# Elementwise work from GpSimd to VectorE and ScalarE, and the later modulation loads on another queue

## The chip, the cores and the metric

The kernel runs on one core of a Trainium2 chip. Its time is the device time of one execution in microseconds (us). Five engines run their own instruction streams in order and wait for one another by semaphores: TensorE (PE; its weight loads are listed as PEld), VectorE (DVE), ScalarE (ACT), GpSimd (POOL) and SyncE (SP), which only issues DMA transfers here. GpSimd issues transfers too, from a queue of its own.

## The reference, cut to what matters

Two transformer blocks, one after the other, on 512 tokens of width 1024 in float32. The first has a recurrent mixer and a sparse attention (projections, rope, softmax branches), then a mixture of 64 experts. The second has two layers of feed-forward, mixer, feed-forward. Both are modulated: vectors computed from a condition `c` scale and shift every normalised activation and scale every residual.

```python
c_act = silu(c)                                  # first block
sh1, sc1, g1, sh2, sc2, g2 = split(c_act @ w_ada[l] + b_ada[l], 6)
h = rmsnorm(x, norm1_g[l]) * (1 + sc1) + sh1
x = x + g1 * (concat([recurrent(h), sparse_attention(h)]) @ w_out[l])
x = x + g2 * moe_ffn(rmsnorm(x, norm2_g[l]) * (1 + sc2) + sh2)

c_act = silu(c_2)                                # second block, two layers
mod = (c_act @ w_mod[l] + b_mod[l]).reshape(9, 1024)
h = modulate(x, g_norm[l, 0], mod[0], mod[1])
x = x + 0.5 * mod[2] * swiglu(h, w_ffn1_gu[l], w_ffn1_down[l])
h = modulate(x, g_norm[l, 1], mod[3], mod[4])
x = x + mod[5] * hybrid_mixer(h, ...)            # window attention, linear recurrence, short convolution
h = modulate(x, g_norm[l, 2], mod[6], mod[7])
x = x + 0.5 * mod[8] * swiglu(h, w_ffn2_gu[l], w_ffn2_down[l])
return rmsnorm(x, g_final)
```

## The kernel before

Matrix products are done to nearly full float32 precision with three passes: every operand is split into a rounded high part and the rest (`split`, lines 164 to 167: ScalarE makes `whi`, VectorE the rest `wlo`), and `mm3` (L160 to L162) adds high by high, high by rest and rest by high. So each piece of 128x1024 weights costs one copy on ScalarE and one subtraction on VectorE before TensorE can use it. Raw weights come over SyncE's queue into three buffers `wraw`; `whi` and `wlo` have three buffers each.

The program runs through four phases. Phase A loads the tokens and normalises them. Phase B makes the projections, the levels of the recurrence (L726 to L790, many small VectorE products on `QP` and `KS`), rope (L386 to L393) and attention (`nsa_cmp`, `nsa_att`). Phase C is the mixture of experts, ended by `moe_end`. Phase D is the second block: `ffn`, `mixer`, `ffn`, twice. In what follows the four feed-forwards are called by layer and place: (0,0), (0,2), (1,0), (1,2).

A modulation vector needs a sum over eight blocks of 128x1024 weights, each scaled by a column of the condition. `mod_acc` (L181) does that: a load of 512 KB into `mraw` (two buffers), then the scaled sum into `macc`, and after eight of them `mod_cols` (L199) adds over the partitions on TensorE (16 small matmuls, L205) and puts the vector into a column tile. It is a generator, and yields after every second block; `tick` (L1442) advances it by one yield at set places of the program: after each pair of column groups in `ffn`, after each slice of `down`, and in phase B after each step of the projections. In phase B (`b_mods`, seven vectors, 56 loads) it runs with `pool=True`: VectorE multiplies the block in place (L189) and GpSimd adds it to the sum (L191). In phase D it runs with `pool=False`: VectorE multiplies and adds in one instruction (L195). Feed-forwards (0,0) and (1,0) carry six vectors each (48 loads), (0,2) carries three (24 loads), (1,2) none.

The order of the instructions on each engine isn't that of the code: a scheduler arranges them ahead of time, by when it takes them to be ready, and `after(ins)` keeps what is issued inside it behind an instruction. `tick` issues its work behind `self.hold`. Before the change `hold` is the last instruction of a normalisation (L1508), so all of a feed-forward's modulation may start at once and is limited by the two `mraw` buffers.

GpSimd also does other elementwise work: the cosine product of rope (L391), a scaling in `hg_norm` (L821), the softmax scaling of every second branch in `nsa_att` (L883) and every second head group in `swa` (L1776), the scaling of `xT` at the end of the experts (L1407), and the running sum of squares of `sq_add` (L1470) for the next normalisation. The page calls the last 256-column part of each feed-forward or output projection `down` with `last`: it is done in two halves of the tokens, and the next normalisation of the first half runs beside the second. It is called the tail here.

Of the kernel before, what the change touches and what calls it, by code (L numbers as in the profile page):

```python
# [19 lines left out]
D = 1024  # L20
# [121 lines left out]
class Kern:  # L142
# [21 lines left out]
    def split(self, src, hi, lo, eng=None):  # L164

        self.copied = self.nc.scalar.copy(hi, src)  # L166
        self.nc.vector.tensor_tensor(lo, src, hi.bitcast(F32), OP.subtract)  # L167
# [13 lines left out]
    def mod_acc(self, src, cact, col0, pool=False):  # L181

        nc = self.nc
        acc = self.m4.tile([128, 1024], F32, name="macc", tag="macc", bufs=3)
        for k in range(8):
            w = self.m4.tile([128, 1024], F32, name="mraw", tag="mraw", bufs=2)
            nc.sync.dma_start(w, src[k * 128:(k + 1) * 128, col0:col0 + 1024])
            if pool:
                nc.vector.tensor_scalar(w if k else acc, w, cact[:, k:k + 1], None, op0=OP.mult)  # L189
                if k:  # L190
                    nc.gpsimd.tensor_tensor(acc, acc, w, OP.add)  # L191
            elif k == 0:
                nc.vector.tensor_scalar(acc, w, cact[:, 0:1], None, op0=OP.mult)
            else:
                nc.vector.scalar_tensor_tensor(acc, w, cact[:, k:k + 1], acc, op0=OP.mult, op1=OP.add)  # L195
            if k % 2:
                yield None
        yield acc
# [164 lines left out]
    def b_consts(self):  # L363
# [10 lines left out]
        nc.gpsimd.tensor_copy(self.cmpm[:].rearrange("p a b -> p (a b)"), tmp[:, 1152:1408])  # L374
# [11 lines left out]
    def rope(self, dst, src):  # L386
        nc = self.nc
        ps = self.bank("pj")
        nc.tensor.matmul(ps, self.rot, src, start=True, stop=True)
        t1 = self.mid.tile([128, S], F32, name="rt", tag="rt", bufs=1)  # L390
        nc.gpsimd.tensor_tensor(t1, src, self.cos, OP.mult)  # L391
        nc.vector.tensor_tensor(dst, ps, self.sin, OP.mult)
        nc.vector.tensor_tensor(dst, dst, t1, OP.add)  # L393

    def b_mods(self):

        yield from self.mod_sub(0, 0, pool=True)
        cols, rows = [], []
        for n in (3, 4, 2, 5):
            for v in self.mod_acc(self.p["w_ada"][0], self.cact, n * D, pool=True):  # L400
                if v is None:
                    yield
# [292 lines left out]
    def hg_inputs(self, win):  # L695
# [14 lines left out]
        with self.after(self.hold):  # L710
            self.b_consts()
        for c in range(2):
# [98 lines left out]
    def hg_norm(self, Gt):  # L811
# [6 lines left out]
        for i in range(4):  # L818
            ov = self.ohg[:, i].rearrange("p (h e) -> p h e", h=4)
            nc.vector.tensor_tensor(ov, ov, ss[:, i, :, None].to_broadcast([128, 4, 128]), OP.mult)  # L820
            nc.gpsimd.tensor_tensor(Gt[:, i], Gt[:, i], ng, OP.mult)  # L821
# [34 lines left out]
    def nsa_att(self, i, g, pct, qr):  # L856
# [11 lines left out]
        for b in range(2):  # L868
# [14 lines left out]
            (nc.gpsimd if b else nc.vector).tensor_tensor(pv, pv, sm[:, :, None].to_broadcast([128, 4, nk]), OP.mult)  # L883
# [444 lines left out]
    def moe_end(self, A, B):  # L1328
# [73 lines left out]
        for h, ps in enumerate((b0, b1)):  # L1402
# [3 lines left out]
            for k in range(0, KT, 4):  # L1406
                nc.gpsimd.tensor_tensor(x[:, k:k + 4], x[:, k:k + 4], t[:, None, :].to_broadcast([128, 4, 256]), OP.mult)  # L1407
# [5 lines left out]
    def mod_sub(self, l, s, pool=False):  # L1413
# [4 lines left out]
        for n in range(3):  # L1418
            col0 = (3 * s + n) * D
            acc = None  # L1420
            for v in self.mod_acc(src, self.cact2, col0, pool):
# [36 lines left out]
    def sq_add(self, k, h):  # L1458
# [10 lines left out]
        elif k < KT - 1:  # L1469
            nc.gpsimd.tensor_tensor(self.ssq, self.ssq, t, OP.add)  # L1470
# [54 lines left out]
    def ffn(self, gu, dn, G, late):  # L1525
# [3 lines left out]
        for gi, nf in enumerate((8, 8, 6)):  # L1529
            n = 0  # L1530
            for pr in range(nf // 2):
# [7 lines left out]
                for j in range(2):  # L1539
# [6 lines left out]
                    n += 1  # L1546
                if n == 4:
# [5 lines left out]
    def down(self, dn, f0, order, G, last):  # L1553
# [6 lines left out]
        for h in range(2 if last else 1):  # L1560
            N = 256 if last else S
            hs = slice(h * 256, h * 256 + N)
            for dp in range(4):
# [17 lines left out]
                for j in range(2):  # L1581
                    k = 2 * dp + j
                    nc.vector.scalar_tensor_tensor(self.xT[:, k, hs], ps[j], G[:, k:k + 1], self.xT[:, k, hs],  # L1583
                                                   op0=OP.mult, op1=OP.add)
# [160 lines left out]
    def swa(self, l, i, q, kk, v, swab):  # L1745
# [27 lines left out]
        for g in range(2):  # L1773
            gp = slice(g * 64, (g + 1) * 64)
            pv = pp[g][:, :, 0:nk]
            (nc.gpsimd if g else nc.vector).tensor_tensor(pv, pv, sm[:, 4 * g:4 * g + 4, None].to_broadcast([128, 4, nk]), OP.mult)  # L1776
# [14 lines left out]
    def phase_d(self):  # L1791
# [6 lines left out]
        for l in range(2):  # L1798
            for s in range(3):
# [3 lines left out]
                self.mg, late = None, self.mods(todo)  # L1803
                if n > 1:
# [33 lines left out]
def body(tc, p, dbg=None, stop=None):  # L1838
    K = Kern(tc, p, dbg, stop)
    PS = bass.MemoryType.PSUM  # L1840
    with tc.tile_pool(name="cst", bufs=1) as K.cp, \
# [6 lines left out]
        K.modc, K.mg, K.hold = {}, None, None  # L1848
        K.banks, K.pj, K.mt = dict(pj=2, sc=3, tr=2, pv=1), "pj", "sc"
# [50 lines left out]
```

## Time and profile before

| | |
|---|---|
| median of 3 runs | 3233.39 us (3231.85 to 3245.57) |
| the profiled execution | 3237.47 us, its span 3235.5 us |
| TensorE busy | 3081.7 us, 95% of the span |
| VectorE busy | 1910.3 us, 59% |
| ScalarE busy | 1237.5 us, 38% |
| GpSimd busy | 507.8 us, 16% |
| mean granted TensorE clock | 0.978 of full speed |

The span is the time from the first to the last instruction; the execution's own time lies 2 us above it. A busy TensorE is not one at its peak: a matmul that runs at half the clock, or whose operands come late, counts as busy for longer. So beside the idle time one has to look at the granted clock, and at how long like work takes in different places. The stages by time: phase A to 56 us, phase B to 520, experts to 1262, the end of the experts to 1300; feed-forwards from 1300, 1889, 2277 and 2860, the two mixers from 1704 and 2674.

### The profile page before, as it was taken

The page shows a single profiled execution, that of the slowest core. Times are in us where ns is not written, and L with a number is a line of the kernel's source. Part 1 is how long each engine was busy: PE and PEld are TensorE (multiplying, and loading weights), DVE is VectorE, ACT ScalarE, POOL GpSimd, SP SyncE. Part 2 cuts the span into 40 slices and gives each one's busy share as a digit, 9 for nine tenths or more (in the row PEclk, how much of TensorE's full clock was granted, in tenths as well). Part 3 has the DMA queues.
Part 4 walks back from the last instruction along what each step waited for, and adds up shares of the span by engine and source line. Part 5 has one row for each costly group of instructions (what it writes and reads, how often), then busy time and mean ns, then how long its engine had stood idle before and what let it go on. Part 6 is the DMA issues. An engine that isn't in the chain of part 4 may idle for free.

```text
span 3235.5 us, 40712 instructions
## 1 busy us (share of the span) xinstructions
PE 3081.7 (95%) x15628; PEld 2347.8 (73%) x15629; DVE 1910.3 (59%) x2962; ACT 1237.5 (38%) x1984; POOL 507.8 (16%) x348
## 2 busy tenths in 40 slices
PE   6998998999999996999999999999999999999999
PEld 5876577555555553777887787888777887788888
DVE  6776757877777766764355674335664355653335
ACT  5123455544454544322245432224322245442223
POOL 0255511222333322100020100001000020100001
PEclk9998899999999998999999999999999999999999
DMA  6555336999899997664243254223664243233223
GB/s 243 165 161 169 98 109 222 315 352 337 301 328 345 331 327 229 214 222 137 93 132 91 91 189 163 91 92 119 204 221 144 93 133 89 79 105 104 96 87 105
DMA packets 317575, 576.58 MB, mean 178 GB/s; under 512 B 49488, under 2 KB 252048, under 8 KB 292800
## 3 DMA queue, kind: packets, MB, share of 16 engines
q1 hardware_dynamic: 294000, 527.27, 47.8%
q0 software_dynamic: 21296, 44.56, 5.6%
q8 instruction: 125, 2.05, 0.3%
q10 hardware_dynamic: 2080, 2.10, 0.2%
q14 instruction: 74, 0.61, 0.1%
HBM read 550.84 MB, written 28.39 MB: 179 GB/s over the span
## 4 chain that ended last, share of the span: by engine, by line
PE 74%; DMA 12%; DVE 8%; issue 3%; ACT 2%; POOL 1%; SPq 0%; DVEq 0%; POOLq 0%; ACTq 0%
PE ps_fm L162 9%; PE ps_fm L161 9%; PE ps_fm L160 9%; DMA mraw<-in_w_mod_dram 8%; PE ps_dn L1322 6%; PE ps_dn L160 5%; PE ps_dn L162 5%; PE ps_dn L161 5%; PE ps_gu L160 3%; PE ps_gu L161 3%; PE ps_gu L162 3%; DVE macc L195 2%; PE ps_tr L1292 2%; PE ps_pj L161 1%; DMA wraw<-in_w_exp_gu_dram 1%
## 5 line engine op out<-in xcount | busy, mean ns | idle before, releaser
L167 DVE TENSOR_TENSOR wlo<-wraw,whi 128x1024 fp32r<-128x1024 f32 x480 | 577.6, 1208 | 570.6 <-ACT whi L166 562.8
L166 ACT CAST whi<-wraw 128x1024 fp32r<-128x1024 f32 x480 | 487.4, 1018 | 857.8 <-PE ps_fm L161 365.9
L160 PE MATMUL ps_fm<-dhh,whi 128*128 128x512 f32 (+1 forms) x1808 | 676.3, 376 | 19.7 <-ACT whi L166 11.6
L162 PE MATMUL ps_fm<-dhh,wlo 128*128 128x512 f32 (+1 forms) x1808 | 666.6, 377 | 15.4 <-DVE wlo L167 15.3
L161 PE MATMUL ps_fm<-dhl,whi 128*128 128x512 f32 (+1 forms) x1808 | 675.2, 375 | 1.8 <-DVE dhl L1508 1.1
L160 PEld LDWEIGHTS ps_fm<-dhh,whi 128*128 128x128 f32 x1808 | 340.2, 189 | 83.6 <-ACT whi L166 13.7
L162 PEld LDWEIGHTS ps_fm<-dhh,wlo 128*128 128x128 f32 x1808 | 340.9, 189 | 80.5 <-DVE wlo L167 20.0
L161 PEld LDWEIGHTS ps_fm<-dhl,whi 128*128 128x128 f32 x1808 | 341.2, 189 | 63.6 <-DVE dhl L1508 4.0
L160 PE MATMUL ps_dn<-ah,whi 128*128 128x256 f32 (+1 forms) x1152 | 384.3, 335 | 1.5 <-DVE xT L1583 1.4
L161 PE MATMUL ps_dn<-al,whi 128*128 128x256 f32 (+1 forms) x1152 | 382.3, 332 | 0.0
L162 PE MATMUL ps_dn<-ah,wlo 128*128 128x256 f32 (+1 forms) x1152 | 382.0, 334 | 0.0
L167 DVE TENSOR_TENSOR wlo<-wbig,whi 128x1024 fp32r<-128x1024 f32 x192 | 231.8, 1219 | 94.3 <-ACT whi L166 94.0
L161 PEld LDWEIGHTS ps_dn<-al,whi 128*128 128x128 f32 x1152 | 216.9, 188 | 25.1 <-issue 1.5
L166 ACT CAST whi<-wbig 128x1024 fp32r<-128x1024 f32 x192 | 198.8, 1047 | 93.2 <-PE ps_gu L162 76.9
L160 PEld LDWEIGHTS ps_dn<-ah,whi 128*128 128x128 f32 x1152 | 216.3, 188 | 24.8 <-DVE xT L1583 2.5
L162 PEld LDWEIGHTS ps_dn<-ah,wlo 128*128 128x128 f32 x1152 | 216.5, 188 | 23.9 <-issue 0.8
L161 PE MATMUL ps_gu<-wlo,th 128*128 128x512 f32 (+21 forms) x512 | 209.7, 409 | 9.7 <-DVE wlo L167 9.7
L160 PE MATMUL ps_gu<-whi,th 128*128 128x512 f32 (+21 forms) x512 | 210.3, 411 | 4.3 <-ACT whi L166 4.2
L1470 POOL TENSOR_TENSOR sq<-sq 128x256 f32<-128x256 f32 x72 | 77.6, 1078 | 856.7 <-issue 721.4
L162 PE MATMUL ps_gu<-whi,tl 128*128 128x512 f32 (+21 forms) x512 | 202.8, 396 | 0.0
L195 DVE SCALAR_TENSOR_TENSOR macc<-mraw,cact,macc 128x1024 f32<-128x1024 f32 x105 | 134.6, 1282 | 105.6 <-DMA mraw<-in_w_mod_dram 104.9
L1583 DVE SCALAR_TENSOR_TENSOR xT<-ps_dn,modc,xT 128x256 f32<-128x256 f32 (+1 forms) x160 | 93.3, 587 | 157.8 <-PE ps_dn L162 156.6
(531 smaller groups left out, 4324.6 us busy)
## 6 DMA issues: line engine op xcount, KB each, us to landing
wbig<-in_w_exp_gu_dram SPq DMA_DIRECT2D x96, 1024.0 KB, 14.2
wraw<-in_w_ffn_gu_dram SPq DMA_DIRECT2D x86, 1024.0 KB, 5.1
mraw<-in_w_mod_dram SPq DMA_DIRECT2D x144, 512.0 KB, 4.3
dnraw<-in_w_exp_dn_dram SPq DMA_DIRECT2D x48, 1024.0 KB, 10.1
wraw<-in_w_exp_gu_dram SPq DMA_DIRECT2D x32, 1024.0 KB, 13.6
wraw<-in_w_ffn_down_dram SPq DMA_DIRECT2D x32, 1024.0 KB, 5.0
wraw<-in_w_out_dram SPq DMA_DIRECT2D x24, 1024.0 KB, 5.0
wraw<-in_w_ffn_down_dram SPq DMA_DIRECT2D x32, 768.0 KB, 4.3
```

Source lines behind the costliest of these rows:

```text
L160: mm(ps, ah, bh, start=first, stop=False)
L161: mm(ps, ah, bl, start=False, stop=False)
L162: return mm(ps, al, bh, start=False, stop=last)
L166: self.copied = self.nc.scalar.copy(hi, src)
L167: self.nc.vector.tensor_tensor(lo, src, hi.bitcast(F32), OP.subtract)
L195: nc.vector.scalar_tensor_tensor(acc, w, cact[:, k:k + 1], acc, op0=OP.mult, op1=OP.add)
L1292: nc.tensor.transpose(ps[:, k * 128:k * 128 + m], g[0:m, 4 * a + k:D:8], self.ident[0:m, 0:m])
L1322: self.mark2 = nc.tensor.matmul(ps[0:m], af[:, k, 0:m], dv[:, k, cs], start=k == 0, stop=k == 1)
L1470: nc.gpsimd.tensor_tensor(self.ssq, self.ssq, t, OP.add)
L1583: nc.vector.scalar_tensor_tensor(self.xT[:, k, hs], ps[j], G[:, k:k + 1], self.xT[:, k, hs], op0=OP.mult, op1=OP.add)
```

## The change

Five things are done together. `mod_acc` loses its split between VectorE and GpSimd: all sums are one VectorE instruction per block. Its loads are issued by GpSimd instead of SyncE, and in the feed-forwards of phase D that carry modulation four more buffers (`mslots`, in the `tok` area that is free then) stand beside the two of `mraw`. `hold` is set anew during a feed-forward: after each pair to the last subtraction of `split`, and in `down` to the update of `xT`. GpSimd's products in rope, `hg_norm`, `moe_end` and `sq_add` go to VectorE. The softmax scalings of `nsa_att` and `swa` become four ScalarE instructions each, one per head.

```diff
-    def mod_acc(self, src, cact, col0, pool=False):
+    def mod_acc(self, src, cact, col0):
         acc = self.m4.tile([128, 1024], F32, name="macc", tag="macc", bufs=3)
         for k in range(8):
-            w = self.m4.tile([128, 1024], F32, name="mraw", tag="mraw", bufs=2)
-            nc.sync.dma_start(w, src[k * 128:(k + 1) * 128, col0:col0 + 1024])
-            if pool:
-                nc.vector.tensor_scalar(w if k else acc, w, cact[:, k:k + 1], None, op0=OP.mult)
-                if k:
-                    nc.gpsimd.tensor_tensor(acc, acc, w, OP.add)
-            elif k == 0:
+            if self.mslots is not None and self.mcount % 6 < 4:
+                w = self.mslots[:, self.mcount % 6]
+            else:
+                w = self.m4.tile([128, 1024], F32, name="mraw", tag="mraw", bufs=2)
+            self.mcount += 1
+            nc.gpsimd.dma_start(w, src[k * 128:(k + 1) * 128, col0:col0 + 1024])
+            if k == 0:
                 nc.vector.tensor_scalar(acc, w, cact[:, 0:1], None, op0=OP.mult)
             else:
                 nc.vector.scalar_tensor_tensor(acc, w, cact[:, k:k + 1], acc, op0=OP.mult, op1=OP.add)
...
# rope
-        nc.gpsimd.tensor_tensor(t1, src, self.cos, OP.mult)
+        nc.vector.tensor_tensor(t1, src, self.cos, OP.mult)
...
# hg_norm
-            nc.gpsimd.tensor_tensor(Gt[:, i], Gt[:, i], ng, OP.mult)
+            nc.vector.tensor_tensor(Gt[:, i], Gt[:, i], ng, OP.mult)
...
# nsa_att (swa alike)
-            (nc.gpsimd if b else nc.vector).tensor_tensor(pv, pv, sm[:, :, None].to_broadcast([128, 4, nk]), OP.mult)
+            if b:
+                for t in range(4):
+                    nc.scalar.mul(pv[:, t], pv[:, t], sm[:, t:t + 1])
+            else:
+                nc.vector.tensor_tensor(pv, pv, sm[:, :, None].to_broadcast([128, 4, nk]), OP.mult)
...
# moe_end
-                nc.gpsimd.tensor_tensor(x[:, k:k + 4], x[:, k:k + 4], t[:, None, :].to_broadcast([128, 4, 256]), OP.mult)
+                with self.after(self.hold):
+                    nc.vector.tensor_tensor(x[:, k:k + 4], x[:, k:k + 4], t[:, None, :].to_broadcast([128, 4, 256]), OP.mult)
...
# sq_add
-            nc.gpsimd.tensor_tensor(self.ssq, self.ssq, t, OP.add)
+            nc.vector.tensor_tensor(self.ssq, self.ssq, t, OP.add)
...
# ffn, after the two column groups of a pair
+                self.hold = self.rest
                 if n == 4:
                     self.mg = late
                 self.tick()
...
# down
-                    nc.vector.scalar_tensor_tensor(self.xT[:, k, hs], ps[j], G[:, k:k + 1], self.xT[:, k, hs],
+                    self.hold = nc.vector.scalar_tensor_tensor(self.xT[:, k, hs], ps[j], G[:, k:k + 1], self.xT[:, k, hs],
...
# phase_d, before each of the six parts
+                self.mslots = self.ap_.tile([128, 4, D], F32, name="mw", tag="tok") if todo else None
```

The scheduler makes a new order from this. On SyncE's queue in phase B, just behind the load of the constants, the loads of weights (`wraw`) and of modulation (`mraw`) stood between one another before:

```order
L187 DMA mraw<-in_w_mod_dram 128x1024 x2
L312 DMA wraw<-in_w_in_dram 128x8x256 x4
L656 DMA wraw<-in_cmp_w_k_dram 128x8x256 x2
L187 DMA mraw<-in_w_mod_dram 128x1024
L656 DMA wraw<-in_cmp_w_v_dram 128x8x256 x2
L187 DMA mraw<-in_w_mod_dram 128x1024 x2
L312 DMA wraw<-in_w_in_dram 128x8x256 x2
L187 DMA mraw<-in_w_mod_dram 128x1024 x2
L425 DMA wraw<-in_w_in_dram 128x8x128 x4
```

Of the change, at the same place, the queue holds the weights alone:

```order
L312 DMA wraw<-in_w_in_dram 128x8x256 x4
L656 DMA wraw<-in_cmp_w_k_dram 128x8x256 x2
L656 DMA wraw<-in_cmp_w_v_dram 128x8x256 x2
L312 DMA wraw<-in_w_in_dram 128x8x256 x2
L425 DMA wraw<-in_w_in_dram 128x8x128 x4
```

All 176 modulation loads of `mod_acc` have left SyncE's queue; on GpSimd's they stand in a row of their own.

On VectorE, in the first group of feed-forward (0,0), between the subtractions for the weights (`wlo`), the products of the two halves of the gate (`si`) and their split (`al`), the sums (`macc`) stood like this before:

```order
L167 TENSOR_TENSOR wlo<-wraw,whi 128x1024
L195 SCALAR_TENSOR_TENSOR macc<-mraw,cact_85,macc 128x1024
L1544 TENSOR_TENSOR si<-si,ps_fm 128x512
L167 TENSOR_TENSOR wlo<-wraw,whi 128x1024
L195 SCALAR_TENSOR_TENSOR macc<-mraw,cact_85,macc 128x1024
L167 TENSOR_TENSOR al<-si,ah 128x512
L195 SCALAR_TENSOR_TENSOR macc<-mraw,cact_85,macc 128x1024 x3
L193 TENSOR_SCALAR macc<-mraw,cact_85 128x1024
L167 TENSOR_TENSOR wlo<-wraw,whi 128x1024
L195 SCALAR_TENSOR_TENSOR macc<-mraw,cact_85,macc 128x1024
```

and now, one pair further on:

```order
L167 TENSOR_TENSOR wlo<-wraw,whi 128x1024 x3
L1550 TENSOR_TENSOR si<-si,ps_fm 128x512
L167 TENSOR_TENSOR al<-si,ah 128x512
L1550 TENSOR_TENSOR si<-si,ps_fm 128x512
L167 TENSOR_TENSOR wlo<-wraw,whi 128x1024
L167 TENSOR_TENSOR al<-si,ah 128x512
L195 SCALAR_TENSOR_TENSOR macc<-mw,cact_85,macc 128x1024 x2
L167 TENSOR_TENSOR wlo<-wraw,whi 128x1024
```

The sums are spread: two stand behind the second `al` of each pair, and none between the others.

On VectorE at the end of the tail of (0,0), where the normalisation's second half begins (`rs`, then `hn` and `dhl`), before:

```order
L1583 SCALAR_TENSOR_TENSOR xT<-ps_dn,modc,xT 128x256 x2
L167 TENSOR_TENSOR wlo<-wraw,whi 128x1024 x2
L238 RECIPROCAL rs<-rs 128x2
L1506 SCALAR_TENSOR_TENSOR hn<-xT,modc,ps_sm 128x256 x3
L1508 SCALAR_TENSOR_TENSOR dhl<-hn,modc,dhh 128x256 x2
```

and now:

```order
L195 SCALAR_TENSOR_TENSOR macc<-mw,cact_85,macc 128x1024
L1514 SCALAR_TENSOR_TENSOR dhl<-hn,modc,dhh 128x256 x2
L195 SCALAR_TENSOR_TENSOR macc<-mw,cact_85,macc 128x1024
L238 RECIPROCAL rs<-rs 128x2
L195 SCALAR_TENSOR_TENSOR macc<-mraw,cact_85,macc 128x1024
L1512 SCALAR_TENSOR_TENSOR hn<-xT,modc,ps_sm 128x256 x3
L195 SCALAR_TENSOR_TENSOR macc<-mraw,cact_85,macc 128x1024
L1514 SCALAR_TENSOR_TENSOR dhl<-hn,modc,dhh 128x256 x3
L195 SCALAR_TENSOR_TENSOR macc<-mw,cact_85,macc 128x1024
```

Before, the sums had all been done by then. Now the last 22 of the 48 stand in the tail and in the normalisation behind it, in (0,0) and in (1,0) alike; the 24 of (0,2) end ahead of its tail.

## Rows read from the trace of the kernel before

**Rows 1.** The page: TensorE's line of part 1, the chain's lines of part 4.

```profile
PE 3081.7 (95%) x15628; PEld 2347.8 (73%) x15629; DVE 1910.3 (59%) x2962; ACT 1237.5 (38%) x1984; POOL 507.8 (16%) x348
...
PE ps_fm L162 9%; PE ps_fm L161 9%; PE ps_fm L160 9%; DMA mraw<-in_w_mod_dram 8%; PE ps_dn L1322 6%; PE ps_dn L160 5%; PE ps_dn L162 5%; PE ps_dn L161 5%; PE ps_gu L160 3%; PE ps_gu L161 3%; PE ps_gu L162 3%; DVE macc L195 2%; PE ps_tr L1292 2%; PE ps_pj L161 1%; DMA wraw<-in_w_exp_gu_dram 1%
```

**Rows 2.** Busy time by stretch; columns in the first line.

```profile
core 0: us, PE busy (x) PEld busy (x) DVE busy (x) ACT busy (x) POOL busy (x), PEclk, DMA share, GB/s
100.00:340.00 240.00, 216.19 (x1372) 182.68 (x1370) 188.88 (x253) 70.37 (x164) 126.25 (x59) 0.91 0.56 168
340.00:460.00 120.00, 117.65 (x594) 63.10 (x595) 70.87 (x109) 59.70 (x134) 39.39 (x21) 0.89 0.26 82
1300.00:1656.00 356.00, 346.58 (x1614) 286.64 (x1613) 184.07 (x202) 94.95 (x124) 11.49 (x6) 1.00 0.49 160
1889.00:2229.00 340.00, 332.98 (x1499) 274.23 (x1500) 144.08 (x162) 90.45 (x111) 0.00 (x0) 0.99 0.39 127
2277.00:2626.00 349.00, 338.51 (x1543) 278.14 (x1542) 172.08 (x188) 90.28 (x112) 1.20 (x2) 1.00 0.49 159
2860.00:3184.00 324.00, 323.44 (x1451) 266.90 (x1452) 116.20 (x131) 89.83 (x111) 0.00 (x0) 1.00 0.29 94
1655.00:1711.00 56.00, 53.00 (x430) 51.60 (x428) 41.82 (x73) 31.23 (x56) 15.68 (x14) 1.00 0.47 141
```

**Rows 3.** VectorE, 60 to 440 us: groups; busy us, mean ns, idle before.

```profile
L189 DVE TENSOR_SCALAR mraw<-mraw,cact 128x1024 f32<-128x1024 f32 x48 | 54.4, 1134 | 31.6 <-DMA mraw<-in_w_ada_dram 19.2 <-DMA mraw<-in_w_mod_dram 12.2
...
L781 DVE TENSOR_TENSOR QP<-QP,ao 128x256 f32<-128x256 f32 x28 | 30.1, 1073 | 0.0
...
L393 DVE TENSOR_TENSOR qr<-qr,rt 128x512 f32<-128x512 f32 x4 | 6.1, 1524 | 2.8 <-POOL rt L391 2.6
L845 DVE TENSOR_TENSOR rc<-rc,gates 128x8 f32<-128x8 f32 x4 | 5.5, 1383 | 0.1
L820 DVE TENSOR_TENSOR o<-o,hss 128x512 f32<-128x512 f32 x4 | 5.5, 1424 | 0.0
...
L392 DVE TENSOR_TENSOR qr<-ps_pj,sin 128x512 f32<-128x512 f32 x4 | 2.7, 682 | 1.5 <-PE ps_pj L389 1.5
...
L778 DVE TENSOR_TENSOR QP<-QP,fT 128x256 f32<-128x256 f32 x4 | 1.6, 409 | 0.0
```

**Rows 4.** Line L189: shortest, median and longest duration in ns.

```profile
L189 DVE TENSOR_SCALAR mraw<-mraw,cact x49: 739/752/2865, 42.5 to 401.5; 128x1024 f32<-128x1024 f32 x49
```

**Rows 5.** GpSimd's groups over the whole span.

```profile
L191 POOL TENSOR_TENSOR macc<-macc,mraw 128x1024 f32<-128x1024 f32 x49 | 124.4, 2540 | 127.8 <-DVE mraw L189 119.1 <-DVE macc L189 7.3 <-DVE mc L206 0.7
...
L883 POOL TENSOR_TENSOR pp<-pp,sm 128x2048 f32<-128x2048 f32 x2 | 7.2, 3601 | 25.1 <-ACT pt L889 16.8 <-DVE sm L881 8.3
```

**Rows 6.** What SyncE's queue waited for, 100 to 340 us (total, times, longest).

```profile
SPq L187 <- POOL macc L191: 127.4, 33, 8.6
```

**Rows 7.** Line L195: shortest, median and longest duration in ns.

```profile
L195 DVE SCALAR_TENSOR_TENSOR macc<-mraw,cact,macc x105: 1273/1284/1289, 1320.8 to 2449.8; 128x1024 f32<-128x1024 f32 x105
```

**Rows 8.** VectorE in order of time, in (1,2): start, duration, idle before.

```profile
3011.20 0.68 DVE L167 TENSOR_TENSOR al<-si,ah 128x512 fp32r<-128x512 f32 x1
3020.95 1.23 DVE L167 TENSOR_TENSOR wlo<-wraw,whi 128x1024 fp32r<-128x1024 f32 x1 [9.06 <-ACT whi L166]
```

**Rows 9.** TensorE in (1,0): the matmuls of one `mod_cols`; start, duration.

```profile
2392.12 1.84 PE L205 MATMUL ps_po<-ones,macc 128*128 128x1 f32 x16
```

**Rows 10.** DMA issues: queue, count, size, median us to landing.

```profile
mraw<-in_w_ada_dram SPq DMA_DIRECT2D x32, 512.0 KB, 3.8
...
x<-in_x_dram POOLq DMA_DIRECT2D x4, 512.0 KB, 5.3
...
acc1d<-sy POOLq DMA_DIRECT2D x4, 512.0 KB, 7.1
```

**Rows 11.** ScalarE: scaling 128x512 in SBUF; busy us, mean ns.

```profile
L284 ACT ACTIVATE xT<-xT,A 128x512 f32<-128x512 f32 x8 | 5.4, 721 | 3.1 <-DVE A L281 3.1
```

More of the change, by code (lines that the diff above doesn't have):

```diff
@@ L166, in split @@
         self.copied = self.nc.scalar.copy(hi, src)
-        self.nc.vector.tensor_tensor(lo, src, hi.bitcast(F32), OP.subtract)
+        self.rest = self.nc.vector.tensor_tensor(lo, src, hi.bitcast(F32), OP.subtract)
     def raw(self):
@@ L373, in b_consts @@
         self.cmpm = bp.tile([128, 4, 64], BF, name="cmpm")
-        nc.gpsimd.tensor_copy(self.cmpm[:].rearrange("p a b -> p (a b)"), tmp[:, 1152:1408])
+        self.hold2 = nc.gpsimd.tensor_copy(self.cmpm[:].rearrange("p a b -> p (a b)"), tmp[:, 1152:1408])
         self.rot = bp.tile([128, 128], F32, name="rot")
@@ L395, in b_mods @@
     def b_mods(self):
-        yield from self.mod_sub(0, 0, pool=True)
+        yield from self.mod_sub(0, 0)
         cols, rows = [], []
         for n in (3, 4, 2, 5):
-            for v in self.mod_acc(self.p["w_ada"][0], self.cact, n * D, pool=True):
+            for v in self.mod_acc(self.p["w_ada"][0], self.cact, n * D):
                 if v is None:
@@ L711, in hg_inputs @@
             self.b_consts()
+        self.hold = self.hold2
         for c in range(2):
@@ L1410, in moe_end, with mod_sub @@
         self.first = 3
-    def mod_sub(self, l, s, pool=False):
+    def mod_sub(self, l, s):
         nc, cp = self.nc, self.cp
@@ L1420, in mod_sub @@
             acc = None
-            for v in self.mod_acc(src, self.cact2, col0, pool):
+            for v in self.mod_acc(src, self.cact2, col0):
                 acc = v
@@ L1582, in down @@
                     k = 2 * dp + j
-                    nc.vector.scalar_tensor_tensor(self.xT[:, k, hs], ps[j], G[:, k:k + 1], self.xT[:, k, hs],
-                                                   op0=OP.mult, op1=OP.add)
+                    self.hold = nc.vector.scalar_tensor_tensor(self.xT[:, k, hs], ps[j], G[:, k:k + 1], self.xT[:, k, hs],
+                                                               op0=OP.mult, op1=OP.add)
                     if last:
@@ L1775, in swa @@
             pv = pp[g][:, :, 0:nk]
-            (nc.gpsimd if g else nc.vector).tensor_tensor(pv, pv, sm[:, 4 * g:4 * g + 4, None].to_broadcast([128, 4, nk]), OP.mult)
+            if g:
+                for t in range(4):
+                    nc.scalar.mul(pv[:, t], pv[:, t], sm[:, 4 + t:5 + t])
+            else:
+                nc.vector.tensor_tensor(pv, pv, sm[:, 0:4, None].to_broadcast([128, 4, nk]), OP.mult)
             pts = []
@@ L1848, in body @@
         K.modc, K.mg, K.hold = {}, None, None
+        K.mslots, K.mcount = None, 0
         K.banks, K.pj, K.mt = dict(pj=2, sc=3, tr=2, pv=1), "pj", "sc"
```

## The prediction

> **What bounds the kernel now.** I read the page's busy shares and its chain of waits first [rows 1]. TensorE is busy for 95% of the span, and nearly all of the chain lies on its matmuls. The two other entries to notice belong to the modulation: its loads (`mraw`) hold 8% of the chain and its sums (L195) 2%. VectorE is busy for 59%, so it matters only where the work stands badly in its order. Next I read busy times by stretch [rows 2], since each part of the change acts in one stage. Two kinds of loss show there. In phase B (the windows 100 to 340 and 340 to 460 us) TensorE is idle for 360 − 216.19 − 117.65 = 26.2 us, and its granted clock of 0.91 and 0.89 costs up to 0.09 × 240 + 0.11 × 120 = 34.8 us more. In phase D the four feed-forwards do the same matrix work but take 356, 340, 349 and 324 us; the last, which carries no modulation, keeps TensorE busy for 323.44 of 324. So modulation costs the others 32, 16 and 25 us. In each view the reader should look for one thing: how long the same instruction, or the same stage, takes with and without the modulation beside it.
>
> **Phase B.** GpSimd's elementwise work goes (126.25 and 39.39 us in the two windows [rows 2], 49 sums of 2540 ns the largest part [rows 5]). VectorE's products beside it take longer than like products elsewhere [rows 3, 4]: L189 has a mean of 1134 ns against a median of 752; L781 takes 1073, where L778 of the same shape takes 409; L393 and L820 take 1524 and 1424, where the 128x512 product of L392 takes 682; L845, a 128x8 product that can't cost more than L778, takes 1383. If all that goes: 48 × 0.382 = 18.3, 28 × 0.664 = 18.6, 4 × 0.842 = 3.4, 4 × 0.742 = 3.0 and 4 × 0.974 = 3.9, together 47.2 us. Against it VectorE takes over the adding: the fused instruction takes 1.284 us [rows 7] in place of 0.752, so 49 × 0.532 = 26.1; the four products of rope and four of `hg_norm` at 0.682 make 5.5 more. Net, VectorE loses 15.6 us of work.
>
> It also waits for modulation loads, 31.6 us [rows 3], and SyncE's queue had waited 127.4 us in 33 pieces for GpSimd's add to free a buffer [rows 6]. That wait goes: a buffer now comes free at the end of VectorE's own instruction. With two buffers still, I take half of the idle time, 16 us. VectorE is busy for 188.88 of 240 us there [rows 2], and TensorE follows it, so I count both: −31.6, rounded to **−30**, since part of TensorE's loss there is its own waiting on other engines. Bounds: the whole idle time and clock loss, −61, on one side; on the other 0, or the loss of the second rival. The DMA issues that leave SyncE's queue leave the loads of weights (`wraw`) behind them earlier, which costs nothing.
>
> **Small edits, −3.** A softmax scaling of 128x2048 took 3.60 us on GpSimd [rows 5]; as four ScalarE instructions of 0.721 [rows 11] it takes 2.9, less where fewer keys are used. ScalarE has 60 us free of 120 in that window [rows 2], so −0 to −1 for each of the few on the path. In `moe_end` the scaling of `xT` goes to VectorE behind the end of the normalisation; at a 1.28 us instruction [rows 7] for GpSimd's 2.5 [rows 5] it may save 1 a piece or cost as much by standing in the queue. −3, with ±5.
>
> **The carrying feed-forwards, −45.** VectorE executes in order, and a sum that waits for its load holds up the `wlo` and `al` behind it that TensorE needs. Now the loads have a queue of their own and six buffers, and two sums stand behind each pair's last `al`. In (1,2) VectorE is idle for 9.06 us at that place [rows 8]; two sums take 2 × 1.284 = 2.57 us, so they cost nothing there. The cover is gone only if a load is late by over 9.06 − 2.57 = 6.5 us. What can be recovered: 16 in (0,2), 25 in (1,0) and 25 in (0,0) (the other 7 of its 32 I put down to the start of the weights behind the experts), 66 us. Not recoverable are the column passes that remain inside, 16 small matmuls in 1.84 us each [rows 9], nine of them: 16.6. Of the 49.4 left I take nine tenths, −45. Bounds: 0, if the loss has another reason, and −66.
>
> **The tails of (0,0) and (1,0), +36.** At two sums a pair the 48 don't fit: 22 come in the tail and the normalisation behind it. Some 20 sums and 2 first products there make 20 × 1.284 + 2 × 0.752 = 27.2 us, and the 14 additions of `sq_add`, which GpSimd did, make at most 14 × 0.409 = 5.7 [rows 3]: 32.9 us on VectorE. In the tail of (0,0) it is busy for 41.82 of 56 us [rows 2], 14.2 free. The rest, 18.7, is late for TensorE, since `hn` and `dhl` stand among the sums in VectorE's order, and the mixer's first matmuls need `dhl`; the three column passes that move there, 3 × 1.84 = 5.5 us, lie beside TensorE's wait. +18 each. Bounds: 0, if TensorE finds other work, and 42 each, if none of the free 14 us is of use (33) and each of the three passes and the sum ahead of it adds 1.84 + 1.284 (9). The tails of (0,2) and (1,2) get the additions alone, 5.7 in 14 free: 0.
>
> **Sum.** −30 − 3 − 45 + 36 = −42, from the profiled 3237.47 us: 3195.5. That execution lies 4.1 above the median of 3233.39; against the median I forecast **3191 us**.
>
> **A rule against the change.** 32 of the loads from SyncE's queue land 3.8 us after issue; two kinds of the same 512 KB from GpSimd's queue take 5.3 and 7.1 [rows 10]. The Trainium skill, in DMA: Bandwidth & Descriptors, section "SWDGE vs HWDGE vs iDMA", says that for transfers issued from GpSimd that engine's cores write descriptors into SBUF, that VectorE can lock it out of that in some modes, and that transfers issued by SyncE are immune. By the same page's "Latency and other measured facts" the first byte comes after about 1 us in place of 0.6; as an estimate from that page, 56 loads would be 56 × 0.4 = 22 us later and the sum −20. No row here shows a first byte or such a lock; the landings agree in sign only, since other transfers ran beside those of 5.3 and 7.1.
>
> **Rivals.**
> - A, no change: the tails cost the upper bound. TensorE waits in both for every sum and its column pass: −30 − 3 − 45 + 2 × 42 = +6, 3239 us. For it: `hn` and `dhl` between sums, with no choice in the order. Against: 14 us free on VectorE there [rows 2].
> - B, slower: the loads of phase B land late. From GpSimd's queue with only two buffers, each comes 5.3 − 3.8 = 1.5 us later [rows 10]; VectorE stands still before the sum, with the products on `QP` and the copies behind it in its order. 56 × 1.5 = 84 us: −42 + 84 = +42, 3275 us. It decides, as slower, once each load costs (42 + 16) / 56 = 1.04 us more. For it: 7.1 us for another load, and the sums stand in short rows there. Against: the buffer comes free earlier by the 2.54 us of an add [rows 5], more than the 1.5, and most of the 127.4 us was waiting for that [rows 6].
> - C, a larger gain: TensorE in phase B recovers its idle time and its clock, since VectorE and the loads were all that held it back: −61 − 3 − 45 + 36 = −73, 3160 us. For it: nearly all of VectorE's excess is beside GpSimd [rows 3, 4]. Against: the granted clock is below full for a part of each window, and TensorE is busy for 117.65 of 120 in the second [rows 2] and could not be given much.
> - That the loads don't run ahead, since four of the buffers lie in an area that is used before: then six are two until it is free, at most a few sums late. I put it inside the forecast's range.
>
> **Numbers.** The forecast has 0.58 (own range 3168 to 3212, about half of the unknown terms either way), A 0.15, C 0.17, B 0.10. A measurement of this kernel can tell about 0.5%, 16 us, from no change. Faster has the forecast and C, 0.75; same A, 0.15; slower B, 0.10. The range reaches from 3148, 12 below C, to 3250, 11 above A; it leaves out B and the far ends of A and C, under 0.2 together.
>
> **What the changed kernel's profile would show.** Right: L781's mean near 0.41 us, no wait of a load's issue for GpSimd's sums, and less idle time on VectorE for `mraw` in phase B; in (1,0) a stretch of some 332 us (349 − 25 × 45 / 66), its sums in the gaps behind `al`; the tails about 74 us, with TensorE waiting for VectorE's `dhl` and `macc`. Wrong: VectorE waits longer for DMA in phase B than 31.6 us (B); tails near 56 + 42 = 98 us (A); (1,0) still near 349 with VectorE free, so that the loss was not the order of the sums.

## The result, and the profile after

The changed kernel takes 3202.43 us (median of 4 runs, 3195.39 to 3208.56) against 3234.59 us for the kernel before (4 runs): a recorded ratio of 0.9894, 95% interval 0.9862 to 0.9925 (the two medians alone make 0.9901). It is faster by about 1.1%; the forecast was 3191 us. The profiled execution took 3204.98 us, with a span of 3203.2 us, 32.3 us less than the span before.

The page's first line and its chain by line, of the changed kernel:

```profile
PE 3079.4 (96%) x15628; PEld 2352.7 (73%) x15629; DVE 1874.3 (59%) x3048; ACT 1263.3 (39%) x2048; POOL 338.8 (11%) x373
...
PE ps_fm L161 12%; PE ps_fm L162 12%; PE ps_fm L160 12%; PE ps_dn L1327 6%; PE ps_dn L160 6%; PE ps_dn L162 6%; PE ps_dn L161 6%; PE ps_gu L160 3%; PE ps_gu L161 3%; PE ps_gu L162 3%; PE ps_sc L876 2%; PE ps_tr L1297 2%; PE ps_pj L161 2%; PE ps_pj L160 2%; PE ps_pj L162 2%
```

Against [rows 1] the loads of `mraw` (8% of the chain) and the sums of L195 (2%) are gone from the lines shown. VectorE is busy for 36 us less, though it has 86 instructions more. The busy time by stretch answers to [rows 2]. The first two windows are the same; from the third on they are shifted to about the same places of the program:

```profile
core 0: us, PE busy (x) PEld busy (x) DVE busy (x) ACT busy (x) POOL busy (x), PEclk, DMA share, GB/s
100.00:340.00 240.00, 232.53 (x1473) 192.98 (x1472) 168.59 (x290) 88.01 (x204) 30.96 (x59) 0.90 0.61 184
340.00:460.00 120.00, 117.25 (x643) 68.41 (x641) 60.87 (x95) 65.75 (x137) 5.26 (x10) 0.92 0.25 85
1280.00:1617.00 337.00, 336.77 (x1574) 280.72 (x1574) 156.55 (x185) 95.26 (x125) 15.92 (x31) 1.00 0.45 144
1874.00:2196.00 322.00, 322.00 (x1451) 265.88 (x1450) 136.95 (x145) 85.73 (x102) 12.67 (x24) 1.00 0.42 134
2249.00:2573.00 324.00, 323.65 (x1465) 267.54 (x1464) 140.74 (x148) 86.38 (x105) 13.74 (x26) 1.00 0.43 137
1617.00:1674.00 57.00, 52.15 (x406) 50.21 (x404) 55.05 (x87) 26.56 (x48) 8.46 (x16) 0.97 0.92 291
```

TensorE is busy for practically all of the carrying feed-forwards, as it was only in (1,2) before. The last row is the tail of (0,0): VectorE is busy for 55.05 of 57 us there, against 41.82 of 56.

One way to see where the time went is to follow a few TensorE instructions that exist in every kernel. The stages below run between such milestones: phases A and B end at the first matmul of the experts (`ps_gu`), and the others go from the first or last matmul of `dhh` by `whi` in one feed-forward to that of another. "Tail + mixer" runs from the last in (0,0) or (1,0) to the first of the next feed-forward. All times are us of one profiled execution each:

| kernel | A+B | experts | (0,0) | tail + mixer | (0,2) | (1,0) | tail + mixer |
|---|---|---|---|---|---|---|---|
| before | 521.3 | 777.5 | 356.0 | 220.7 | 353.1 | 362.6 | 220.7 |
| changed | 503.2 | 776.9 | 337.3 | 235.4 | 343.1 | 342.0 | 239.7 |
| difference | −18.1 | −0.6 | −18.7 | +14.7 | −10.0 | −20.6 | +19.0 |

The seven differences make −34.3; the tail of (0,2), the end of the program and (1,2) add back 1.3, 0.6 and 0.1, which is the 32.3 of the span.

Two stages are worth a closer look. A window less TensorE's busy time is its idle time. These are phases A and B, before and changed (columns as above):

```profile
0.00:521.30 521.30, 467.41 (x2737) 361.20 (x2738) 360.23 (x540) 215.90 (x431) 178.65 (x103) 0.93 0.50 159
0.00:503.20 503.20, 464.76 (x2737) 358.83 (x2738) 318.24 (x549) 231.01 (x463) 48.73 (x92) 0.94 0.51 164
```

TensorE's idle time went from 53.9 to 38.4 us, 15.5 less, and VectorE's busy time from 360.23 to 318.24, 42.0 less. And this is the tail of (0,0) with its mixer, before and changed, and the 45 us behind the mixer's first matmul in the changed kernel:

```profile
1654.80:1875.50 220.70, 216.87 (x1363) 180.95 (x1362) 145.45 (x229) 112.92 (x220) 36.26 (x36) 1.00 0.36 109
1617.40:1852.80 235.40, 226.13 (x1403) 188.69 (x1402) 171.07 (x275) 118.89 (x235) 16.61 (x34) 0.98 0.46 147
1654.90:1699.90 45.00, 38.98 (x256) 36.04 (x256) 39.41 (x67) 17.36 (x30) 6.17 (x9) 0.89 0.57 153
```

The 14.7 us have three parts. TensorE is idle for 9.3 us in place of 3.8. It makes 40 more matmuls, two and a half column passes, 4.6 us at 1.84 each [rows 9]. And its granted clock falls to half (1.2 GHz) for some us, behind waits for `macc`, `dhl` and `dhh`: 0.89 over those 45 us, a loss of 0.11 × 45 = 5.0 us. That makes 15.1. In the tail of (1,0) it is idle for 10.2 us in place of 3.8; behind a wait of 3.26 us for `macc` the clock over the like 45 us is 0.81, a loss of 8.6. With the same 4.6 for the passes that makes 19.6, where the stage grew by 19.0.

VectorE's groups in the changed kernel, 60 to 440 us (busy us, mean ns, idle before):

```profile
L195 DVE SCALAR_TENSOR_TENSOR macc<-mraw,cact,macc 128x1024 f32<-128x1024 f32 x49 | 62.8, 1281 | 24.5 <-DMA mraw<-in_w_ada_dram 16.3 <-DMA mraw<-in_w_mod_dram 8.1
...
L782 DVE TENSOR_TENSOR QP<-QP,ao 128x256 f32<-128x256 f32 x28 | 11.6, 416 | 0.3 <-PE ps_tr L754 0.3
...
L193 DVE TENSOR_SCALAR macc<-mraw,cact 128x1024 f32<-128x1024 f32 x7 | 5.2, 750 | 2.6 <-DMA mraw<-in_w_ada_dram 2.5
...
L393 DVE TENSOR_TENSOR qr<-qr,rt 128x512 f32<-128x512 f32 x4 | 2.7, 686 | 0.0
...
L846 DVE TENSOR_TENSOR rc<-rc,gates 128x8 f32<-128x8 f32 x4 | 0.7, 164 | 0.0
```

The products that were long beside GpSimd in [rows 3] have the duration of their like: the product on `QP` takes 416 ns (1073 before), `qr` 686 (1524), `rc` 164 (1383). What did not go is the wait for loads: 24.5 + 2.6 us, of 31.6 before. GpSimd's queue shows why (what it waited for, 100 to 340 us; total, times, longest):

```profile
POOL mraw L191 <- DVE macc L195: 130.5, 37, 8.7
POOL mraw L191 <- DVE macc L193: 33.8, 5, 19.3
```

SyncE's queue had waited 127.4 us for GpSimd's sums [rows 6]. Now GpSimd's queue waits as long for VectorE's: with two buffers each load still has to wait for a sum, only for another engine's.

### The profile page after: what moved, and what is told of

Same layout as the page of the kernel before. It is cut to its first block, busy times and chain, and to the rows that moved or that the text cites. A ratio compares the mean times of both kernels' runs of the same rounds, so it can differ in the third digit from the quotient of the medians.

```text
span 3203.2 us, 40592 instructions
## 1 busy us (share of the span) xinstructions
PE 3079.4 (96%) x15628; PEld 2352.7 (73%) x15629; DVE 1874.3 (59%) x3048; ACT 1263.3 (39%) x2048; POOL 338.8 (11%) x373
## 3 DMA queue, kind: packets, MB, share of 16 engines
q0 software_dynamic: 46640, 136.84, 14.7%
## 4 chain that ended last, share of the span: by engine, by line
PE 85%; DVE 5%; DMA 5%; issue 3%; ACT 1%; POOL 0%; SPq 0%; DVEq 0%; ACTq 0%; POOLq 0%
PE ps_fm L161 12%; PE ps_fm L162 12%; PE ps_fm L160 12%; PE ps_dn L1327 6%; PE ps_dn L160 6%; PE ps_dn L162 6%; PE ps_dn L161 6%; PE ps_gu L160 3%; PE ps_gu L161 3%; PE ps_gu L162 3%; PE ps_sc L876 2%; PE ps_tr L1297 2%; PE ps_pj L161 2%; PE ps_pj L160 2%; PE ps_pj L162 2%
## 5 line engine op out<-in xcount | busy, mean ns | idle before, releaser
L167 DVE TENSOR_TENSOR wlo<-wraw,whi 128x1024 fp32r<-128x1024 f32 x480 | 566.4, 1183 | 656.3 <-ACT whi L166 649.7
L161 PEld LDWEIGHTS ps_fm<-dhl,whi 128*128 128x128 f32 x1808 | 343.4, 190 | 64.3 <-DVE dhl L1514 4.6
L1327 PE MATMUL ps_dn<-dnraw,eaf 128*80 128x512 f32 (+20 forms) x368 | 167.4, 596 | 0.5 <-ACT eaf L976 0.5
L1198 POOL DMA_INDIRECT ring<-h2d,iidx x64 | 96.0, 1500 | 381.6 <-PE ps_tr L1297 130.3
```

Of the source, the lines that this page charges most:

```text
L161: mm(ps, ah, bl, start=False, stop=False)
L167: self.rest = self.nc.vector.tensor_tensor(lo, src, hi.bitcast(F32), OP.subtract)
L1198: self.nc.gpsimd.indirect_dma_start(out=g[0:cap], out_offset=None, in_=self.h2d[:], in_offset=bass.IndirectOffsetOnAxis(ap=i_ap[0:cap], ax ...
L1327: self.mark2 = nc.tensor.matmul(ps[0:m], af[:, k, 0:m], dv[:, k, cs], start=k == 0, stop=k == 1)
```

## The experiments

Eleven kernels were run, each an edit of the changed kernel. The four with several runs are compared with the kernel before in runs on the same chip; the others were run once, and are read from their traces by the milestones above.

**Modulation loads back on SyncE's queue (spq).**

```diff
-            nc.gpsimd.dma_start(w, src[k * 128:(k + 1) * 128, col0:col0 + 1024])
+            nc.sync.dma_start(w, src[k * 128:(k + 1) * 128, col0:col0 + 1024])
```

> The changed kernel with one thing undone: the 176 modulation loads are issued by SyncE's queue again, still into six buffers in the feed-forwards; sums and their places as changed. Theory (the places of the sums made the feed-forwards faster, and GpSimd leaving the adding made phase B faster; the queue matters little): each carrying feed-forward within 4 us of the changed kernel, phase B ending within 6 us of its 503 us, 3195 to 3212 us in all. Rival (loads on their own queue made it): the feed-forwards give back 10 us or more each and phase B ends 8 us or more later, 3230 us or more.

3204.84 us (4 runs), ratio to before 0.9898 [0.987, 0.9927], as the changed kernel's 0.9894. The stages: phases A and B 504.5, then 339.1, 343.2 and 342.0 in the feed-forwards, all inside the theory's bounds. With six buffers and the places there, the queue is worth next to nothing in the whole time. A small effect shows in phase B: TensorE's idle time there is 43.6 us, 42.4 and 43.2 in the other two kernels with these loads on SyncE's queue (s6n and s2h, below), and 38.0 to 41.1 in the six kernels whose phase B is the changed one's. (With the queue the scheduler's order in phase B changes too, so the two aren't told apart.)

**Phase B's modulation as before (bpool).**

```diff
-            nc.gpsimd.dma_start(w, src[k * 128:(k + 1) * 128, col0:col0 + 1024])
-            if k == 0:
+            (nc.sync if pool else nc.gpsimd).dma_start(w, src[k * 128:(k + 1) * 128, col0:col0 + 1024])
+            if pool:
+                nc.vector.tensor_scalar(w if k else acc, w, cact[:, k:k + 1], None, op0=OP.mult)
+                if k:
+                    nc.gpsimd.tensor_tensor(acc, acc, w, OP.add)
+            elif k == 0:
...
# b_mods: both calls with pool=True
```

> The changed kernel with the modulation of phase B alone as before: loads on SyncE's queue, product on VectorE, sum on GpSimd; rope, the attention and phase D as changed. Theory (GpSimd's sums beside VectorE's products were the cost): L782 and its like rise from 0.42 to about 1 us again, the load's issue waits over 100 us for GpSimd's sums, and phase B ends 13 to 18 us later than the 503 us of the changed kernel; 3216 to 3222 us. Rival (rope, hg_norm and the softmax scaling made the gain of phase B): phase B ends within 5 us of 503, about 3203 us.

3229.91 us (10 runs), 0.9982 [0.9963, 1.0001]. Phase B ends at 522.1 us, 18.9 later than the changed kernel's 503.2 and about where it was before (521.3); TensorE is idle for 58.4 us there, against 38.4. VectorE's product on `QP` is long again, and SyncE's queue waits for GpSimd's sums (VectorE's group, 60 to 440 us; the queue, 100 to 340 us):

```profile
L786 DVE TENSOR_TENSOR QP<-QP,ao 128x256 f32<-128x256 f32 x28 | 30.5, 1090 | 0.0
```

```profile
SPq L191 <- POOL macc L195: 132.0, 33, 8.5
```

So taking the 49 sums from GpSimd is what gained in phase B; spq has shown that the queue, undone here with it, isn't the cause. In this kernel rope and `hg_norm` have left GpSimd and the softmax scalings stand on ScalarE, and that alone gained nothing there that one execution shows. The end is a little later than the 13 to 18 us that were expected.

**No places for the sums in the feed-forwards (nohold).**

```diff
-                self.hold = self.rest
...
-                    self.hold = nc.vector.scalar_tensor_tensor(self.xT[:, k, hs], ps[j], G[:, k:k + 1], self.xT[:, k, hs],
+                    nc.vector.scalar_tensor_tensor(self.xT[:, k, hs], ps[j], G[:, k:k + 1], self.xT[:, k, hs],
```

> The changed kernel without the new places of hold in feed-forwards: as before all sums of a feed-forward may start at its normalisation; queue, six buffers and all else as changed. The order then has nearly all sums in the first group of each feed-forward and its down, and none in the tails. Theory (the places made the gain of some 48 us in the three feed-forwards and the loss of some 33 us in the two tails): feed-forwards give back 35 to 48, the tails give 28 to 33, so 3202 to 3222 us in all. Rival (six buffers and the queue made the feed-forwards faster; the places only cost the tails): feed-forwards as in the changed kernel within 4 us each, tails short, about 3170 us.

3174.54 us (4 runs), 0.9809 [0.9778, 0.9839]: the rival's value, 28 us below the changed kernel. Feed-forwards 343.0, 343.4 and 346.8; tails with mixers 220.7 both, as before the change. The theory, that the places made the gain, was wrong: they are not needed for it, and they are the whole loss in the tails. (0,0) and (1,0) are 5.7 and 4.8 us longer than in the changed kernel; that is about the three column passes that come back into each (3 × 1.84 = 5.5 [rows 9]).

**Sums early, none in the tail (early).**

```diff
                 self.tick()                 # ffn, behind a pair
+                if self.six:
+                    self.tick()
...
                 self.tick()                 # down
+                if self.six and not last:
+                    self.tick()
...
+                self.six = len(todo) == 2   # phase_d
```

> The changed kernel with two ticks instead of one behind each pair, and in down of the first two groups, of (0,0) and (1,0): the sums come four behind a pair and all 48 end ahead of the tail. Theory (the tail lost its time to 22 sums on a full VectorE, and the gap behind a pair has room for 9.06 us of work, four sums are 5.1): tails back to their old length, -14 and -17 us to -19, feed-forwards slower by 0 to 3 each, 3166 to 3176 us. Rival (four sums in a row delay the subtractions for the weights): feed-forwards give back 10 or more each, 3190 us or more.

3173.74 us (6 runs), 0.9798 [0.9773, 0.9823]. Tails with mixers 219.9 and 219.8. In the tail of (0,0) and its mixer VectorE has room again, TensorE is idle for 3.3 us, and the granted clock stays at 1.00 (columns as above):

```profile
1621.10:1841.00 219.90, 216.59 (x1355) 180.03 (x1354) 146.44 (x248) 118.89 (x235) 7.02 (x16) 1.00 0.38 119
```

The feed-forwards take 343.1, 343.1 and 347.4, so (0,0) and (1,0) are 5.8 and 5.4 us slower, where 0 to 3 were expected: the three column passes that come back into each, 5.5 us, had been left out. Four sums in a row behind a pair delay nothing beyond them. This kernel and the one without places are about equal, and both beat the changed kernel and the one before.

**Buffers, places and queue taken apart (p2n, s6n, p2h, s2h).** The kernels above left open which of the three made the feed-forwards faster. Each of these edits joins two or three of the small ones: `nohold`'s for "no places", `spq`'s for "SyncE", and for two buffers

```diff
-                self.mslots = self.ap_.tile([128, 4, D], F32, name="mw", tag="tok") if todo else None
+                self.mslots = self.ap_.tile([128, 4, D], F32, name="mw", tag="tok") if False else None
```

> The changed kernel without the places of hold and with two modulation buffers throughout; loads from GpSimd's queue. Feed-forwards (0,0) and (1,0), first matmul to last pair, took 356 and 362 us before, 337 and 342 changed, 343 and 347 without the places (six column passes more inside). Theory (VectorE stands still at sums whose loads are late, since with two buffers the third load waits for the first sum): 354 to 358 and 360 to 364, VectorE's wait for modulation loads in (0,0) 40 us or more again. Rival (loads on SyncE's queue held up the weights): 341 to 345 and 345 to 349.

> The changed kernel without the places of hold, its loads on SyncE's queue, six buffers. Theory (VectorE stands still at sums whose loads are late; six buffers cure it): (0,0) and (1,0) 341 to 346 and 345 to 350 us. Rival (loads on SyncE's queue hold up the weights): 350 us or more and 355 us or more.

> The changed kernel with two modulation buffers throughout; places of hold and GpSimd's queue kept. Theory (late loads at sums bunched together were the cost, so either cure does): two sums a pair leave 22 us for two loads, so (0,0) and (1,0) stay within 3 us of 337 and 342. Rival (the lead of six buffers is what counts, wherever the sums stand): 345 us or more and 350 us or more.

> The changed kernel with two modulation buffers throughout and its loads on SyncE's queue; only the places of hold differ from the kernel before in the feed-forwards. Theory (late loads at sums bunched together were the cost, so either cure does): (0,0) and (1,0) within 4 us of 337 and 342. Rival (SyncE's queue, blocked by a load that waits for its buffer, holds up the weights): 345 us or more and 350 us or more, with TensorE waiting for whi and wlo.

One run each: 3189.65, 3185.69, 3199.9 and 3218.54 us, beside 3233.48 for the kernel before. The feed-forwards in us, with the kernels told already; "no places" has all six column passes inside (0,0) and all six inside (1,0) (in some kernels half of the last one falls behind the end), "places" three each. The first row is the kernel before itself, which differs from the changed one in the small edits too:

| | (0,0) | (0,2) | (1,0) |
|---|---|---|---|
| no places, two buffers, SyncE (before) | 356.0 | 353.1 | 362.6 |
| no places, two buffers, GpSimd (p2n) | 350.9 | 347.0 | 350.2 |
| no places, six buffers, SyncE (s6n) | 343.1 | 343.3 | 347.6 |
| no places, six buffers, GpSimd (nohold) | 343.0 | 343.4 | 346.8 |
| places, two buffers, SyncE (s2h) | 337.2 | 343.2 | 342.0 |
| places, two buffers, GpSimd (p2h) | 337.5 | 343.2 | 342.0 |
| places, six buffers, GpSimd (changed) | 337.3 | 343.1 | 342.0 |

Six buffers are a full cure, on either queue, and so are the places, with two buffers on either queue. Only where neither is there does the queue count: with two buffers and no places, the loads on GpSimd's queue save 5.1, 6.1 and 12.4 us. For p2n, in (0,0) and in (1,0), the theory's bounds were too high and the rival's too low; late loads at the sums and the queue each have a part. (s2h is long as a whole for its tails with mixers, 239.2 and 248.9.) What VectorE waited for in (0,0), of the kernel before, of p2n, and of nohold (total, times, longest):

```profile
DVE wlo L167 <- ACT whi L166: 83.1, 28, 9.9
DVE macc L195 <- DMA mraw<-in_w_mod_dram: 43.8, 26, 4.8
```

```profile
DVE macc L195 <- DMA mraw<-in_w_mod_dram: 37.2, 28, 3.2
```

```profile
DVE macc L195 <- DMA mw<-in_w_mod_dram: 1.6, 3, 1.0
```

The large row is no loss: VectorE waits for `whi` because it is ahead. The row to read is `macc`: some 40 us of standing still at sums with two buffers, almost none with six. Most of that costs TensorE nothing: (0,0) is 13.0 us longer than in nohold in the kernel before, and 7.9 in p2n. How SyncE's queue adds its part where there are two buffers and no places was not looked into.

**A quarter of phase B's modulation (bfew).**

```diff
-        for k in range(8):
+        for k in range(8 if self.pj == "fm" else 2):
```

> The changed kernel, but in phase B each modulation sum covers two of its eight blocks (14 loads and sums in place of 56; the modulation vectors of that phase are then wrong). The changed phase B, up to the first matmul of the experts, ended at 494.7 to 503.2 us in five executions, median 497.8. Theory (what the forecast of -30 was short by is still the modulation: 24.5 us of VectorE's waiting for its loads and 68 us of sums): it ends 8 to 25 us earlier than 497.8. Rival (modulation now costs TensorE nothing there; the rest is the low clock and waits of the attention's own): within 4 us of 497.8.

This kernel leaves out six of the eight blocks of every sum in phase B. 3190.68 us in one run. Phase B ends at 489.6 us. The six profiled executions whose phase B has the changed kernel's instructions in the same order (changed, nohold, early, p2n, p2h, sqpool) end it at 494.7 to 506.5, median 498.4; so this is 8.8 us earlier (8.2 by the median recorded ahead of it), the lower edge of what the theory asked for. Its trace doesn't bear the theory out:

```profile
0.00:489.60 489.60, 452.83 (x2737) 352.85 (x2738) 270.55 (x508) 229.74 (x463) 26.36 (x50) 0.97 0.38 124
```

VectorE has 47.7 us less to do than in the changed kernel, but TensorE's idle time is 36.8 us, against 38.0 to 41.1 in the six. The rest is that the same 2737 matmuls keep it busy for less, 452.83 us (455.88 to 466.99 in the six), at a granted clock of 0.97. So of the modulation that is left, three quarters cost TensorE 1 to 4 us of idle time. Whether the edit raised the clock as well can't be told from one run.

**Additions of `sq_add` back on GpSimd (sqpool).**

```diff
-            nc.vector.tensor_tensor(self.ssq, self.ssq, t, OP.add)
+            nc.gpsimd.tensor_tensor(self.ssq, self.ssq, t, OP.add)
```

> The changed kernel with the additions of sq_add on GpSimd again. Theory (in the tails of (0,0) and (1,0) VectorE is the bound, so every instruction counts there, and nowhere else): last pair of (0,0) to first matmul of (0,2), 236 us in the changed kernel, and of (1,0) to (1,2), 240, become 3 to 6 us shorter; the tails of (0,2) and (1,2) within 1 us. Rival (the additions lie in slack or GpSimd is as late with them): all within 2 us.

3216.92 us in one run. Tails with mixers 241.8 and 241.2 (235.4 and 239.7 in the changed kernel), so not shorter: the theory is wrong on that, and the additions are not what makes the tails long. The tail of (0,2) does get back its 34.1 us (35.4 changed). The 6.4 us by which the stage behind (0,0) is longer are 1.8 of idle time (11.1 against 9.3) and 4.6 of TensorE's busy time for like matmuls, at a granted clock of 0.96 against 0.98. The clock can move this stage by several us between kernels that leave it alone; it took 238.8 in the next one.

**Softmax scalings back on GpSimd (smpool).**

```diff
-            if b:
-                for t in range(4):
-                    nc.scalar.mul(pv[:, t], pv[:, t], sm[:, t:t + 1])
-            else:
-                nc.vector.tensor_tensor(pv, pv, sm[:, :, None].to_broadcast([128, 4, nk]), OP.mult)
+            (nc.gpsimd if b else nc.vector).tensor_tensor(pv, pv, sm[:, :, None].to_broadcast([128, 4, nk]), OP.mult)
# swa alike
```

> The changed kernel with the softmax scalings of nsa_att and swa on GpSimd again, in one instruction each. Forecast's term (0 to -1 us each, within -3): phase B ends 0 to 6 us later than the 497.8 of the changed kernel (five executions, 494.7 to 503.2), and the mixers within 2 us. Rival (ScalarE, which makes the exponentials and copies for the attention, is the later engine, so the four instructions cost more than they save): phase B ends 5 us or more earlier, the mixers 1 to 4 us shorter.

3201.96 us in one run; phase B ends at 495.2, inside the range of the six executions; tails with mixers 238.8 and 236.9. Neither the forecast's term nor the rival can be told from this.

## Why the prediction was right, and where it was off

The time lies in the range, and the balance of gains against a loss in the tails was the measured one: −42 was forecast, the spans of the two profiled executions differ by −32.3. Not every term was right for its reason.

- **Phase B: −30 forecast, −18.1 measured**, and −22.9 with the median 498.4 of the six executions. That GpSimd's sums were the cause was right: bpool shows it. The sum behind the −30 was not. VectorE's work was put 15.6 us lower and came out 42.0 lower. The groups reckoned with were about as computed (the product on `QP` 18.5 us, of 18.6), but others had been longer beside GpSimd too, such as `sm` of the softmax: 16 products that took 533 ns each and now 161. Of the 31.6 us idle on loads half was to go, and 4.5 went, since the buffers still come free only behind a sum. Above all, VectorE's time was counted as TensorE's, one for one. VectorE gained some 46 us, and TensorE's idle time fell by 15.5. That this lies beside the 15.6 is chance. bfew shows the same from the other side.
- **Small edits: −3 forecast, −0.6** in the stage of the experts, which took 776.0 to 781.7 in the other kernels, and nothing told apart by smpool.
- **Feed-forwards: −45 forecast, −49.3 measured** (18.7 + 10.0 + 20.6). The cause named was right, VectorE standing still at sums whose loads are late. But the prediction put it down to queue, buffers and places together, and the runs show that six buffers or the places alone do it. The size owes something to luck. The 32 us of (0,0) come from windows that start 1 us behind that feed-forward's first matmul, but some 14 us behind it in the three others. Between the milestones (1,2) takes 337.7, so the loss was 18.3, 15.4 and 24.9. The same sum from there, 58.6 in place of 66, makes −38. It was made up for because (1,2) is no floor: (0,0), with three column passes, ended 6 us below 337.7 + 5.5.
- **Tails: +36 forecast, +33.7 measured** (14.7 + 19.0), all of it given back once the sums end earlier (nohold, early). That the sums fill VectorE there was right (55.05 of 57 us). The parts were others. VectorE's excess was to make TensorE 18.7 us late each time, with the column passes beside that wait. TensorE's idle time grew by 5.5 and 6.4 us only, the passes added 4.6 of their own, and the fallen clock cost 5.0 and 8.6, for which the sum had no term. So the total is near in part by luck. Nor does sqpool bear out the price of the additions. The 1.3 us that the tail of (0,2) lost had been put at 0.
- **Rival B** (loads from GpSimd's queue land late in phase B) had the wrong sign. Its landings were later indeed: the 32 loads for the first block's vectors took 4.3 us, against 3.8 [rows 10]. But VectorE waited less, and the three kernels with the loads on SyncE's queue end phase B at 500.6, 503.0 and 504.5, not earlier than the six with a median of 498.4, with TensorE idle for 42.4 to 43.6 us against 38.0 to 41.1. The Trainium skill's first-byte figures for the two kinds of queues, weighed in the prediction (DMA: Bandwidth & Descriptors, "Latency and other measured facts"), differ by 0.4 us; the landings here differ by 0.5, which is in line with that, though no trace shows a first byte; no stage shows a cost.
- **Rival A** (the tails cost 42 each) was too dear, and **rival C** (−61 in phase B) out of reach: even bfew, at a higher clock, gained 31.7.

## What to carry to other kernels

An elementwise instruction on GpSimd is not free for being off the busy engines: here VectorE's product on `QP` took 2.6 times as long beside its sums, a small product 8 times, and moving the 124 us of sums to VectorE made VectorE less busy. But time saved on an engine that isn't the bottleneck isn't time saved on the one that is: of some 46 us on VectorE a third reached TensorE. Where a stream of loads feeds sums that stand among urgent work on an engine that runs in order, either give it the buffers to be ahead or place the sums in the gaps; here one of the two was enough. A spread that doesn't finish ahead of the next full stretch gives part of the gain away again (33.7 of 49.3 us here), so count the gaps against the sums first.

## What the runs showed of the hardware

The end of phase B varied by 12 us between executions of the same instructions, and went with the granted clock. These rows are for sqpool and p2n, whose phase B is the changed kernel's; they end it at 506.5 and 494.7 us (columns as above):

```profile
0.00:506.50 506.50, 466.99 (x2736) 360.68 (x2737) 318.92 (x549) 231.54 (x463) 48.70 (x92) 0.93 0.50 163
0.00:494.70 494.70, 455.88 (x2737) 353.47 (x2738) 318.10 (x550) 230.63 (x463) 48.59 (x92) 0.96 0.51 167
```

TensorE's idle time is almost the same, 39.5 and 38.8 us. Of the 11.8 us between the ends 11.1 are busy time for the same matmuls, at a clock of 0.93 and 0.96. So an edit of a few us in this stage can't be read from where one execution ends it; the idle time varies less, from 38.0 to 41.1 us over the six. The kernel before had 0.93 as well and ended 14.8 us later than sqpool, with 14.4 us more of idle time. So 14 to 15 us is what this pair shows of the change at one clock. That the rest of the −22.9 is clock fits these rows, but was not tested by itself.

The clock fell in the tails too, where the sums made TensorE wait: to 0.89 and 0.81 over 45 us, against 1.00 in nohold and early, where these waits are gone. That the waits bring the fall fits all these runs; no run changed one without the other.
